# Four edits to the order of work in the scan layer of a decoder trunk: the spread roots go through SBUF, the sums of squares, the casts of y and the turned x change places

## The chip, the cores and the metric

The kernel runs on one core of one Trainium2 chip. The metric is the device time of one execution in microseconds (us), the median of several runs of the same program. The engines are named as the profile names them: PE is the matrix engine (PEld its weight loads), DVE the vector engine, ACT the scalar engine, POOL the general engine, and SP the engine whose queue issues most of the loads.

## What is computed

Two layers of a decoder trunk on 256 tokens of width 1024, all in float32. Each layer is a SwiGLU feed-forward, a token mixer and a second feed-forward, each followed by a layer norm. The first layer's mixer is sparse attention, the second's is a Mamba-2 scan in two chunks of 128 tokens. The change touches the scan layer alone. Cut to what matters there:

```
z, xbc, dt = split(x @ w_in)                    # z: 2048 wide, x: 2048, B and C: 4 groups of 128
xbc = silu(conv(xbc));  xs, b, c = split(xbc)
decay = exp(where(tri, a_cs[l] - a_cs[s], -inf))
y  = (cb * decay) @ (xs * dt)                   # within a chunk, and from chunk 0 to chunk 1
y  = y + xs * d_skip
yz = y * silu(z)                                # 4 groups g of 512 channels
yz = yz * rsqrt(mean(yz ** 2, over the group) + eps)
out = (yz * norm_g) @ w_out
```

## The kernel before, in words

**Precision.** A float32 product is made of three fast ones: every operand is split into a high part H (a cast) and a low part L (the rest), and `mm3` (L565 to L568) adds H·H, H·L and L·H in PSUM. For each weight tile ("unit") a load brings `raw`, ACT casts it to `wh` (L352, or L350 with a scale), and DVE subtracts to make `wl` (L380, L377); for a few units ACT and a DMA that adds (L358, L359) make `wl` instead. Up to ten units are kept ready ahead of PE, and four raws are on their way in this layer.

**The scan layer is turned.** Everything stands with channels on the partitions and tokens along the row. It runs in four stages, g = 0 to 3, one for each group of 512 channels, and each engine carries out its instructions in exactly the order in which the program writes them. To keep PE busy, each stage has up to eight *fillers* f[0] to f[7]: pieces of projection work that depend on nothing in the stage. In stages 0 and 1, f[0] to f[3] compute and convolve the next group's x (`xs_tile`, 24 products, tiles `pxs` or `pmm`), and f[4] to f[7] compute a group of z (`z_tile`, 24 products into one of two PSUM banks `pmm`, freed when ACT has taken silu of it at L1561). In stage 2 there are four x tiles and four output pieces (`out_piece`, 12 products with 512 columns), in stage 3 six output pieces. Between the fillers stand the steps of the stage:

- `x_tok` (L1658 on) transposes x of a group back to tokens on PE (L1666) and multiplies by dt on DVE (L1668); `x_end` multiplies by the decay to the chunk's end (L1672). `decay_cbs` multiplies the three decay tiles M by C·B (L1652).
- `diag` (48 products in the trace, L1685) makes y of the group in two PSUM banks called `ptr`. There are only two such banks; they go round among `diag`, `x_tok`, `root` and `spread`.
- `gate` (DVE, L1695 and L1700) adds the skip and multiplies by silu(z), giving `yc`. `squares` (ACT, L1704) squares it, and `square_sum` (DVE, L1709, L1710) folds the four channel tiles into one.
- `root` sums over the partitions on PE (L1716), copies the two columns out (ACT, L1718) and takes the power -0.5 (POOL, L558).
- One stage later `spread` puts the roots along the rows of a `ptr` bank with two products on PE (L1725), `norm` multiplies `yc` by them on DVE straight out of that bank (L1734) and casts the result to yH on ACT (L1737), and `norm_low` makes yL on DVE (L1741). The output pieces need yH and yL.
- `decay_load` issues the loads of the next stage's decay tiles on POOL's queue, `decay_seg` (DVE, L1639) and `decay_exps` (ACT, L1646) turn them into decays. `flush` issues the silu of the last convolved tile (ACT, L1590); `W.lows()` and `W.pump()` issue the parts of the next weights.

The exponential and the silu each need a table on ACT, so that a table load stands ahead of the exponentials and another ahead of the next silu.

Of the kernel before, what the change touches and what calls it, by code (L numbers as in the profile page):

```python
# [74 lines left out]
def ffn_steps(seven):  # L75
# [3 lines left out]
    while j < NJ:  # L79
        kind, n = ('S', 4) if j in seven else ('R', 1)  # L80
        j += n
# [355 lines left out]
def trunk_kernel(ctx: ExitStack, tc: tile.TileContext, widths, forms, x, ln_g, ln_b, wts, kvg, convp,  # L437
                 dt_bias, a_log, d_skip, norm_g, out):
    nc = tc.nc
# [10 lines left out]
    def nm(s):  # L450
        cnt[0] += 1
        return f"{s}_{cnt[0]}"

    def f4(s):
        return wk.tile([128, 1024], F32, name=nm(s), tag="f4", bufs=12)

    def f2(s):
        return wk.tile([128, 512], F32, name=nm(s), tag="f2", bufs=11)

    def f1(s):  # L460
        return wk.tile([128, 256], F32, name=nm(s), tag="f1", bufs=6)

    def r2(s):
        return wk.tile([128, 512], F32R, name=nm(s), tag="r2", bufs=10)

    def tiny(s, n=32):
        return wk.tile([128, n], F32, name=nm(s), tag=f"tiny{n}", bufs=14 if n == 32 else 4)
# [4 lines left out]
    def pmm():  # L472
        return psum.tile([128, 512], F32, name=nm("pmm"), tag="pmm", bufs=2)
# [11 lines left out]
    def ptr():  # L485
        return psum.tile([128, 512], F32, name=nm("ptr"), tag="ptr", bufs=2)
# [67 lines left out]
    def rsqrt_pool(src):  # L554

        n = src.shape[1]
        o = tiny("rs")
        nc.gpsimd.tensor_tensor(o[:, :n], src, mhalf.to_broadcast([128, n]) if n > 1 else mhalf, op=ALU.pow)  # L558
        return o[:, :n]
# [891 lines left out]
    def ssd(xT, u, ln_i):  # L1451
# [102 lines left out]
        def z_tile(g, i, uu):  # L1554

            if not i:
                zT[g] = f4("zT")
            ps = pmm()
            proj_b(ps[:, :256], xT, uu, False)
            W.free(uu)  # L1560
            nc.scalar.activation(zT[g][:, i * 256:(i + 1) * 256], ps[:, :256], AF.Silu)  # L1561
            W.pump(1)
# [25 lines left out]
        def flush():  # L1588
            while late:
                nc.scalar.activation(*late.pop(0), AF.Silu)  # L1590
# [40 lines left out]
        def hv(ap):  # L1631
            return ap.rearrange("p (h d) -> p h d", h=8)

        def hb(ap, g):
            return ap[:, g * 8:(g + 1) * 8][:, :, None].to_broadcast([128, 8, 64])

        def decay_seg(t, g):

            nc.vector._custom_dve(TENSOR_ADD_SAT, out=M[t].rearrange("p (h l) -> p h l", h=8),  # L1639
                                  in0=M[2 * t].rearrange("p (h l) -> p h l", h=8),  # L1640
                                  in1=acs[t][:, g * 8:(g + 1) * 8][:, :, None].to_broadcast([128, 8, 128]),
                                  s0=0.0, s1=LOWEST)

        def decay_exps():
            for m in (M[0], M[2], M[1]):
                nc.scalar.activation(m, m, AF.Exp)  # L1646
# [7 lines left out]
        yT = {}  # L1654
        y, xe, yc, sq = {}, {}, {}, {}

        def x_tok(t, g):

            if t:
                pt = ptr()  # L1660
            elif g < 3:
                pt = psum.tile([128, 512], F32, name=nm("pxt"), tag="acc11", bufs=1)
            else:
                pt = pmm()
            for i in range(4):
                nc.tensor.transpose(pt[:, i * 128:(i + 1) * 128], xsT[g][i][:, t * 128:(t + 1) * 128], ident)  # L1666
            y[t] = f2("xdt")
            nc.vector.tensor_mul(hv(y[t]), hv(pt), hb(dt[:, t * 32:(t + 1) * 32], g))  # L1668

        def x_end(g):  # L1670
            xe[g] = f2("xe")
            nc.vector.tensor_mul(hv(xe[g]), hv(y[0]), hb(dend, g))  # L1672
# [17 lines left out]
        def gate(g, py):  # L1690
            yc[g] = f4("yc")
            sq[g] = [f2("sq"), f2("sq")]
            for b in range(2):
                for i in (2 * b, 2 * b + 1):
                    nc.vector.scalar_tensor_tensor(yc[g][:, i * 256:(i + 1) * 256], xsT[g][i],  # L1695
                                                   dsk[:, 4 * g + i:4 * g + i + 1],
                                                   py[b][:, (i % 2) * 256:(i % 2 + 1) * 256],
                                                   op0=ALU.mult, op1=ALU.add)
                c = slice(b * 512, (b + 1) * 512)
                nc.vector.tensor_mul(yc[g][:, c], yc[g][:, c], zT[g][:, c])  # L1700
# [5 lines left out]
        def square_sum(g):  # L1706

            a, b = sq[g]
            nc.vector.tensor_add(a, a, b)  # L1709
            nc.vector.scalar_tensor_tensor(b[:, :256], a[:, :256], 4 * RMS_EPS, a[:, 256:], op0=ALU.add, op1=ALU.add)  # L1710

        def root(g):

            pt = ptr()
            for t in range(2):
                nc.tensor.matmul(pt[:, t:t + 1], sq[g][1][:, t * 128:(t + 1) * 128], mean, start=True, stop=True)  # L1716
            ms = tiny("ss")
            nc.scalar.copy(ms[:, :2], pt[:, :2])  # L1718
            return rsqrt_pool(ms[:, :2])

        def spread(rs):

            pt = ptr()
            for t in range(2):
                nc.tensor.matmul(pt[:, t * 128:(t + 1) * 128], rs[:, t:t + 1].to_broadcast([128, 128]), ident,  # L1725
                                 start=True, stop=True)
            return pt[:, :256]

        def norm(g, rs):
            R = spread(rs)  # L1730
            yT[g] = [(r2("yH"), r2("yL")) for _ in range(2)]
            vs = [yc[g][:, b * 512:(b + 1) * 512] for b in range(2)]
            for v in vs:
                nc.vector.tensor_mul(v.rearrange("p (i l) -> p i l", i=2), v.rearrange("p (i l) -> p i l", i=2),  # L1734
                                     R[:, None, :].to_broadcast([128, 2, 256]))
            for (H, L), v in zip(yT[g], vs):
                nc.scalar.copy(H, v)  # L1737

        def norm_low(g):
            for b, (H, L) in enumerate(yT[g]):  # L1740
                nc.vector.tensor_sub(L, yc[g][:, b * 512:(b + 1) * 512], H.bitcast(F32))  # L1741

        def xs_tile(g, i, uu):
            if not i:
                xsT[g] = []
            ps = xbank() if g < 3 else pmm()
            proj_b(ps[:, :256], xT, uu, False)
            W.free(uu)
            if not i % 2:
                pair[0] = f2("xsT")  # L1750
            o = pair[0][:, (i % 2) * 256:(i % 2 + 1) * 256]
            conv(ps, g * 4 + i, o)
            xsT[g].append(o)
            W.pump(1)
# [56 lines left out]
        for g in range(SG):  # L1811
            if g < 2:
                f = [lambda i=i: xs_tile(g + 1, i, u + i) for i in range(4)]
                f += [lambda i=i: z_tile(g + 2, i, u + 4 + i) for i in range(4)]
            elif g == 2:
                x3 = [lambda i=i: xs_tile(3, i, u + 2 * i) for i in range(4)]
                o0 = [lambda i=i: out_piece(i, u + 2 * i + 1) for i in range(4)]
                f = [x3[0], x3[1], o0[0], x3[2], o0[1], x3[3], o0[2], o0[3]]
            else:
                f = [lambda i=i: out_piece(4 + i, u + i) for i in range(6)]  # L1820
            if g:
                x_tok(0, g)
                x_tok(1, g)
            x_end(g)
            decay_cbs(g)
            f[0]()
            if not g:
                z_turn(1)
            if g == 3:
                norm(2, rs)  # L1830
                f[1]()
                py = diag(3)
                gate(3, py)
                squares(3)
                norm_low(2)
                f[2]()
                square_sum(3)
                f[3]()
                rs = root(3)
                f[4]()  # L1840
                norm(3, rs)
                norm_low(3)
                f[5]()
                continue
            f[1]()
            if g:
                norm(g - 1, rs)
            f[2]()
            py = diag(g)
            for t in range(2):  # L1850
                decay_load(t, g + 1)
            if g:
                norm_low(g - 1)
            W.lows()
            gate(g, py)
            f[3]()
            squares(g)
            f[4]()
            flush()
            square_sum(g)  # L1860
            f[5]()
            rs = root(g)
            decay_seg(0, g + 1)
            f[6]()
            flush()
            decay_seg(1, g + 1)
            decay_exps()
            f[7]()
            u += 8
        u += 6  # L1870
# [47 lines left out]
```

## Time and profile before

| what | value |
|---|---|
| median of 3 runs | 1018.83 us (1018.36 to 1019.18) |
| the profiled execution | 1019.94 us |
| its span, first to last instruction | 1018.2 us |
| mean granted clock of PE | 0.993 |
| busy: PE, DVE, ACT, POOL | 98%, 90%, 65%, 10% of the span |
| the four stages of the scan, on PE | about 701 to 814 us of the span |

The trace is of one execution. In the rows of the timeline the columns are start in us, length in us, engine, line, operation, tiles written and read, and in brackets how long the engine had been idle before and whose end it waited for. Matmuls overlap in the pipeline, so that a stretch's length from start to start says more than the sum of its parts. The lines are those of the kernel before.

### The profile page before, as it was taken

The numbers are of one execution on the slowest core, as the hardware profiler recorded it, in microseconds if no ns is written. First come the engines' busy times: TensorE is split into PE (matmuls) and PEld (weight loads), VectorE is DVE, ScalarE is ACT, GpSimd is POOL, SyncE is SP. The second block draws the span as 40 slices with busy tenths as digits, with TensorE's granted clock in tenths as the row PEclk, the third lists the DMA queues.
The fourth block names the chain that finished last, engine by engine and source line by source line (L and its number), as shares of the span: only waits on it lengthen the run. The fifth ranks groups of instructions, "written<-read, shape, count | busy, mean of one in ns | idle before, by whom it ended". The sixth has DMA issues, their size and how long they took to land.

```text
span 1018.2 us, 14875 instructions
## 1 busy us (share of the span) xinstructions
PE 1001.6 (98%) x5445; PEld 851.9 (84%) x5445; DVE 913.2 (90%) x1242; ACT 661.3 (65%) x953; POOL 106.4 (10%) x152
## 2 busy tenths in 40 slices
PE   9999999999999999999999999999989999999996
PEld 7888888898788888888888888999989788888885
DVE  6999998789899999989999998697778999999985
ACT  6776775476657676754777664587757555776670
POOL 0111101100001110000011000150110001010000
PEclk9999999999999999999999999999989999999998
DMA  9989999352638998882999886447686664999751
GB/s 342 281 249 284 297 275 345 105 173 75 214 106 242 253 280 285 267 304 75 266 254 263 278 292 232 164 143 205 205 233 194 225 225 114 292 294 292 207 187 42
DMA packets 64953, 230.66 MB, mean 227 GB/s; under 512 B 7312, under 2 KB 8144, under 8 KB 64880
## 3 DMA queue, kind: packets, MB, share of 16 engines
q1 hardware_dynamic: 52128, 183.95, 50.1%
q0 software_dynamic: 12752, 45.76, 22.5%
q8 instruction: 42, 0.69, 0.3%
q14 instruction: 31, 0.25, 0.1%
HBM read 193.48 MB, written 1.08 MB: 191 GB/s over the span
## 4 chain that ended last, share of the span: by engine, by line
PE 85%; DVE 6%; ACT 3%; issue 2%; DMA 2%; POOL 1%; SPq 0%; DVEq 0%; ACTq 0%; POOLq 0%
PE pmm L566 12%; PE pmm L568 12%; PE pmm L567 12%; PE acc L566 9%; PE acc L568 9%; PE acc L567 9%; PE ptr L567 2%; PE ptr L568 2%; PE ptr L566 2%; DVE wl L380 2%; PE pmm L733 1%; PE ptr L834 1%; DMA raw<-raw 1%; PE ptr L733 1%; PE pxs L566 1%
## 5 line engine op out<-in xcount | busy, mean ns | idle before, releaser
L352 ACT CAST wh<-raw 128x1024 fp32r<-128x1024 f32 (+2 forms) x433 | 430.2, 1039 | 121.4 <-DVE raw L318 78.8
L380 DVE TENSOR_TENSOR wl<-raw,wh 128x1024 fp32r<-128x1024 f32 (+3 forms) x421 | 491.4, 1208 | 14.5 <-ACT wh L352 13.5
L566 PE MATMUL acc<-wh,hH 128*128 128x512 f32 (+1 forms) x352 | 138.0, 392 | 0.0
L567 PE MATMUL acc<-wl,hH 128*128 128x512 f32 (+1 forms) x352 | 136.7, 388 | 0.0
L568 PE MATMUL acc<-wh,hL 128*128 128x512 f32 (+1 forms) x352 | 136.7, 388 | 0.0
L566 PE MATMUL pmm<-wh,xT 128*128 128x512 f32 (+2 forms) x280 | 108.9, 389 | 0.0
L568 PE MATMUL pmm<-wh,xT 128*128 128x512 f32 (+2 forms) x280 | 107.5, 384 | 0.0
L567 PE MATMUL pmm<-wl,xT 128*128 128x512 f32 (+2 forms) x280 | 107.4, 384 | 0.0
L291 POOL DMA_DIRECT2D raw<-raw x59 | 50.8, 876 | 401.2 <-DVE raw L318 233.1
L566 PE MATMUL pmm<-wh,xf 128*128 128x512 f32 x224 | 87.9, 392 | 0.0
L567 PE MATMUL pmm<-wl,xf 128*128 128x512 f32 x224 | 87.3, 390 | 0.2 <-DVE wl L380 0.2
L568 PE MATMUL pmm<-wh,xf 128*128 128x512 f32 x224 | 87.3, 390 | 0.0
L318 DVE TENSOR_TENSOR raw<-raw,raw 128x1024 f32<-128x1024 f32 x69 | 82.9, 1219 | 0.4
L567 PEld LDWEIGHTS acc<-wl,hH 128*128 128x128 f32 x352 | 66.2, 188 | 13.6 <-DVE wl L380 0.8
L568 PEld LDWEIGHTS acc<-wh,hL 128*128 128x128 f32 x352 | 66.1, 188 | 13.7
L566 PEld LDWEIGHTS acc<-wh,hH 128*128 128x128 f32 x352 | 66.2, 188 | 12.9
L568 PEld LDWEIGHTS pmm<-wh,xT 128*128 128x128 f32 x280 | 52.6, 188 | 11.0 <-DVE xT L563 0.9
L567 PEld LDWEIGHTS pmm<-wl,xT 128*128 128x128 f32 x280 | 52.7, 188 | 10.1 <-DVE wl L380 0.8
L566 PEld LDWEIGHTS pmm<-wh,xT 128*128 128x128 f32 x280 | 52.6, 188 | 9.7 <-ACT xT L562 0.4
L567 PEld LDWEIGHTS pmm<-wl,xf 128*128 128x128 f32 x224 | 42.1, 188 | 9.1 <-DVE wl L380 0.6
L568 PEld LDWEIGHTS pmm<-wh,xf 128*128 128x128 f32 x224 | 42.0, 188 | 8.8
L566 PEld LDWEIGHTS pmm<-wh,xf 128*128 128x128 f32 x224 | 42.1, 188 | 8.6
(346 smaller groups left out, 1936.2 us busy)
## 6 DMA issues: line engine op xcount, KB each, us to landing
raw<-in_wts_dram SPq DMA_DIRECT2D x338, 512.0 KB, 5.3
raw<-raw POOLq DMA_DIRECT2D x59, 512.0 KB, 6.1
M<-scr POOLq DMA_DIRECT2D x8, 512.0 KB, 6.2
wl<-raw POOLq DMA_DIRECT2D x8, 512.0 KB, 5.6
lng<-in_ln_g_dram POOLq DMA_DIRECT2D x6, 512.0 KB, 5.6
lnb<-in_ln_b_dram POOLq DMA_DIRECT2D x6, 512.0 KB, 5.3
raw<-in_wts_dram SPq DMA_DIRECT2D x4, 408.0 KB, 5.5
raw<-in_wts_dram SPq DMA_DIRECT2D x4, 256.0 KB, 3.9
```

Source lines behind the costliest of these rows:

```text
L291: self.nc.gpsimd.dma_start(self.raw[r], self.raw[other], accum_op=ALU.add)
L318: self.nc.vector.tensor_add(self.raw[r], self.raw[r], self.raw[other])
L352: nc.scalar.copy(h[:, c:c + n], raw[:, c:c + n])
L380: self.nc.vector.tensor_sub(lo[:, s], raw[:, s], h[:, s].bitcast(F32))
L566: nc.tensor.matmul(ps, lh, rh, start=first, stop=False, skip_group_check=on)
L567: nc.tensor.matmul(ps, lh, rl, start=False, stop=False, skip_group_check=on)
L568: nc.tensor.matmul(ps, ll, rh, start=False, stop=last, skip_group_check=on)
L733: nc.tensor.matmul(ps, H[:, k * 128:(k + 1) * 128], xT.HL[:, k, :], start=k == 0, stop=False)
L834: nc.tensor.transpose(pt[:, i * 256 + t * 128:i * 256 + (t + 1) * 128], h[:, i * 128:(i + 1) * 128], ident)
```

## The change

It makes four edits, all in the scan layer:

1. `spread` copies the roots from the `ptr` bank into a small SBUF tile R on ACT (L1728 of the changed kernel), and DVE multiplies by R instead of by the bank.
2. The casts to yH leave `norm` for a function of their own. In stages 1 and 2 they are issued behind `diag` and the loads of the decay; `norm_low`, which subtracts them, moves behind `gate`. In stage 3 `norm_low(2)` moves behind `square_sum(3)`.
3. `root` of stages 0 to 2 is issued behind f[6] rather than behind f[5].
4. `x_tok` and `x_end` of the next group are issued at the end of a stage, ahead of f[7], rather than at the start of the next one, behind f[7].

```
-            return pt[:, :256]
+            R = f1("R")
+            nc.scalar.copy(R, pt[:, :256])
+            return R
...
-            R = spread(rs)
+            R = rs if rs.shape[1] == 256 else spread(rs)
...
-            for (H, L), v in zip(yT[g], vs):
-                nc.scalar.copy(H, v)
+
+        def norm_high(g):
+            for b, (H, L) in enumerate(yT[g]):
+                nc.scalar.copy(H, yc[g][:, b * 512:(b + 1) * 512])
...
-            if g:
-                x_tok(0, g)
-                x_tok(1, g)
-            x_end(g)
+            if not g:
+                x_end(g)
...
                 norm(2, rs)
+                norm_high(2)
...
                 squares(3)
-                norm_low(2)
                 f[2]()
                 square_sum(3)
+                norm_low(2)
...
             if g:
-                norm_low(g - 1)
+                norm_high(g - 1)
             W.lows()
             gate(g, py)
+            if g:
+                norm_low(g - 1)
             f[3]()
             squares(g)
             f[4]()
             flush()
             square_sum(g)
             f[5]()
-            rs = root(g)
             decay_seg(0, g + 1)
             f[6]()
             flush()
+            rs = root(g)
             decay_seg(1, g + 1)
             decay_exps()
+            x_tok(0, g + 1)
+            x_tok(1, g + 1)
+            x_end(g + 1)
             f[7]()
```

(`rs` always has two columns here, so that `norm` always calls `spread`.)

Three places in the order of the built programs follow. The numbers behind the names tell buffers apart and differ a little between the two programs.

PE, end of stage 1, before: the last products of f[5], the sums over the partitions (L1716), and the first products of f[6].

```order
L566 MATMUL pmm_7602<-xT_6170,wh_7340 128x256
L567 MATMUL pmm_7602<-xT_6170,wh_7340 128x256
L568 MATMUL pmm_7602<-xT_6170,wl_7341 128x256
L1716 MATMUL ptr_7633<-mean,sq_7521 128x1 x2
L566 MATMUL pmm_7641<-xT_6170,wh_7396 128x256
```

PE, end of stage 1, now: the last products of f[6], the sums, the eight transposes of group 2's x (L1666), and the first product of f[7].

```order
L567 MATMUL pmm_7636<-xT_6170,wh_7396 128x256
L568 MATMUL pmm_7636<-xT_6170,wl_7397 128x256
L1716 MATMUL ptr_7668<-mean,sq_7521 128x1 x2
L1666 MATMUL pxt_7679<-ident,xsT_7387 128x128 x2
L1666 MATMUL pxt_7679<-ident,xsT_7473 128x128 x2
L1666 MATMUL ptr_7686<-ident,xsT_7387 128x128 x2
L1666 MATMUL ptr_7686<-ident,xsT_7473 128x128 x2
L566 MATMUL pmm_7695<-xT_6170,wh_7434 128x256
```

So the sums have moved 24 products later, and the transposes 24 products earlier.

DVE, middle of stage 1, before: the product of y with the roots, the convolution of f[2]'s tile (`cv_7474`), low parts of weights (`wl`), yL, and the gate of this stage.

```order
L1734 TENSOR_TENSOR yc_7152<-yc_7152,ptr_7437 128x512 x2
L1598 SCALAR_TENSOR_TENSOR cv_7474<-pxs_7448,convp_sb,cv_7474 128x255
L1598 SCALAR_TENSOR_TENSOR cv_7474<-pxs_7448,convp_sb,cv_7474 128x254
L1598 SCALAR_TENSOR_TENSOR cv_7474<-pxs_7448,convp_sb,cv_7474 128x253
L380 TENSOR_TENSOR wl_7435<-raw_7301,wh_7434 128x1024
L1741 TENSOR_TENSOR yL_7441<-yc_7152,yH_7440 128x512
L1741 TENSOR_TENSOR yL_7443<-yc_7152,yH_7442 128x512
L380 TENSOR_TENSOR wl_7484<-raw_7338,wh_7483 128x1024
L1695 SCALAR_TENSOR_TENSOR yc_7519<-xsT_7023,dsk,ptr_7486 128x256 x2
L1700 TENSOR_TENSOR yc_7519<-yc_7519,zT_7034 128x512
L1695 SCALAR_TENSOR_TENSOR yc_7519<-xsT_7108,dsk,ptr_7487 128x256 x2
L1700 TENSOR_TENSOR yc_7519<-yc_7519,zT_7034 128x512
```

The same place now:

```order
L1736 TENSOR_TENSOR yc_7152<-yc_7152,R_7440 128x512 x2
L1598 SCALAR_TENSOR_TENSOR cv_7474<-pxs_7448,convp_sb,cv_7474 128x255
L1598 SCALAR_TENSOR_TENSOR cv_7474<-pxs_7448,convp_sb,cv_7474 128x254
L1598 SCALAR_TENSOR_TENSOR cv_7474<-pxs_7448,convp_sb,cv_7474 128x253
L380 TENSOR_TENSOR wl_7435<-raw_7294,wh_7434 128x1024
L380 TENSOR_TENSOR wl_7484<-raw_7354,wh_7483 128x1024
L1695 SCALAR_TENSOR_TENSOR yc_7519<-xsT_7023,dsk,ptr_7486 128x256 x2
L1700 TENSOR_TENSOR yc_7519<-yc_7519,zT_7034 128x512
L1695 SCALAR_TENSOR_TENSOR yc_7519<-xsT_7108,dsk,ptr_7487 128x256 x2
L1700 TENSOR_TENSOR yc_7519<-yc_7519,zT_7034 128x512
L1745 TENSOR_TENSOR yL_7443<-yc_7152,yH_7442 128x512
L1745 TENSOR_TENSOR yL_7445<-yc_7152,yH_7444 128x512
```

The two yL stand behind the gate, and the first row reads R instead of a PSUM bank. What stands between that row and the sum of squares has the same length as before; only its order is another.

ACT, middle of stage 1, before: the last weight cast of f[1], the casts of y, and what convolves f[2]'s tile (`cv_7474`).

```order
L352 CAST wh_7434<-raw_7301 128x1024
L1737 CAST yH_7440<-yc_7152 128x512
L1737 CAST yH_7442<-yc_7152 128x512
L1595 ACTIVATE cv_7474<-pxs_7448,convp_sb 128x256
L1590 ACTIVATE xsT_7387<-cv_7426 128x256
L352 CAST wh_7483<-raw_7338 128x1024
```

And now:

```order
L352 CAST wh_7434<-raw_7294 128x1024
L1728 COPY R_7440<-ptr_7437 128x256
L1595 ACTIVATE cv_7474<-pxs_7448,convp_sb 128x256
L1590 ACTIVATE xsT_7387<-cv_7426 128x256
L352 CAST wh_7483<-raw_7354 128x1024
L1741 CAST yH_7442<-yc_7152 128x512
```

The copy of the roots takes the place of the two casts, and the casts stand behind f[2]'s convolution and its weight cast.

More of the change, by code (lines that the diff above doesn't have):

```diff
@@ L1841, in ssd @@
                 norm(3, rs)
+                norm_high(3)
                 norm_low(3)
```

## The prediction

> **What bounds the kernel now.** I read the page first, then the table of the waits of PE between 690 and 815 us, then PE's timeline around each of them, and last the timelines of DVE and ACT, to see why they were late.
>
> ```profile
> span 1018.2 us, 14875 instructions
> PE 1001.6 (98%) x5445; PEld 851.9 (84%) x5445; DVE 913.2 (90%) x1242; ACT 661.3 (65%) x953; POOL 106.4 (10%) x152
> ```
>
> PE is the bound, and it is full almost everywhere. So only stretches in which it stands still, or runs slower than the same work elsewhere, can be won. The waits of PE in the scan have three rows, 5.8 us in all:
>
> ```profile
> PE ptr L1716 <- DVE sq L1710: 3.0, 2, 2.5
> PE ptr L1685 <- DVE yc L1734: 2.4, 2, 1.4
> PE pmm L566 <- ACT zT L1561: 0.4, 1, 0.4
> ```
>
> The windows of PE give what they cost, start to start. The columns are the length of the stretch, PE's busy time with its instructions, the granted clock, and DMA.
>
> ```profile
> 712.24:715.01 2.77, 2.77 (x49) 1.00 0.53 101
> 723.75:729.95 6.20, 6.20 (x54) 1.00 0.76 207
> 729.95:730.75 0.80, 0.80 (x11) 1.00 0.97 343
> 739.98:743.96 3.98, 2.99 (x49) 1.00 0.82 210
> 752.70:755.34 2.64, 0.16 (x3) 1.00 0.60 213
> 755.34:764.63 9.29, 9.29 (x52) 0.63 0.84 222
> 765.42:771.91 6.49, 6.08 (x51) 1.00 0.20 74
> 786.94:792.49 5.55, 5.55 (x26) 1.00 0.82 321
> 799.40:803.95 4.55, 3.16 (x50) 1.00 0.34 115
> 803.95:810.16 6.21, 5.74 (x26) 1.00 0.83 291
> ```
>
> The first three rows are undisturbed: `diag` of stage 0 takes 2.77 us, `root` with two fillers 6.20, the eight transposes 0.80; so is the eighth, two output pieces of stage 2 in 5.55. The same `diag` takes 3.98 in stage 1 and 4.55 in stage 3. In stage 1 `root` comes 2.64 us late (fifth row), and then `root` with its two fillers takes 9.29 instead of 6.20, at a mean granted clock of 0.63 (sixth row). That row is busy throughout: the matmuls themselves are slower.
>
> **Part by part.** The sum is made against the profiled execution, 1019.94 us (its span of 1018.2 and 1.74 around it); that is 1.11 above the median of 1018.83, and I take the difference off the median.
>
> *The roots through SBUF.* In stages 1 and 3 the second bank of `diag` is the one that `spread` filled, and PE stands until DVE has multiplied by it:
>
> ```profile
> 742.50 0.33 PE L1685 MATMUL ptr<-M,xdt 128*64 128x128 f32 x2 [0.99 <-DVE yc L1734]
> 802.49 0.33 PE L1685 MATMUL ptr<-M,xdt 128*64 128x128 f32 x2 [1.39 <-DVE yc L1734]
> 739.74 1.03 ACT L352 CAST wh<-raw 128x1024 fp32r<-128x1024 f32 x1
> 741.79 1.22 ACT L1737 CAST yH<-yc 128x512 fp32r<-128x512 f32 x2 [1.01 <-DVE yc L1734]
> L982 ACT COPY gate<-pmm x5: 373/373/385, 34.2 to 978.6; 128x256 f32<-128x256 f32 x5
> ```
>
> The trace has no copy of the roots; its nearest row is L982, the same shape out of PSUM, 0.37 us. Four of them are 1.5 us on ACT, which idles 1.01 us here ahead of the casts whose place the copy takes. In stage 1 the copy follows the cast that ends at 740.77, so that the bank is free near 741.1; `diag` starts at 739.98 and reaches its second half 1.4 us later. Gain 3.98 - 2.77 = 1.21, at worst 0.9 if the copy is 0.3 late. In stage 3 the cover is as good, but the gain depends on DVE, below.
>
> ```profile
> L1734 DVE TENSOR_TENSOR yc<-yc,ptr x8: 672/678/689, 741.1 to 814.7; 128x512 f32<-128x512 f32 x8
> L1709 DVE TENSOR_TENSOR sq<-sq,sq x4: 683/686/693, 722.2 to 808.9; 128x512 f32<-128x512 f32 x4
> ```
>
> The multiply itself I cost at no change: out of PSUM it takes 678 ns, the same shape out of SBUF alone 686. [...]
>
> *The casts behind the diagonal products, the sums a filler later.* What makes `root` late in stage 1 is DVE, and DVE had itself been held up:
>
> ```profile
> 743.51 1.51 DVE L1598 SCALAR_TENSOR_TENSOR cv<-pxs,convp_sb,cv 128x255 f32<-128x255 f32 x3 [1.15 <-ACT cv L1595]
> ...
> 754.76 0.43 DVE L1710 SCALAR_TENSOR_TENSOR sq<-sq 128x256 f32<-128x256 f32 x1
> 755.34 0.90 PE L1716 MATMUL ptr<-mean,sq 128*128 128x1 f32 x4 [2.48 <-DVE sq L1710]
> ```
>
> The 1.15 us of idle come from ACT: the casts to yH wait for the product, and the convolution of the next tile stands behind them. With the casts moved, DVE goes straight on, and its sum of squares is done at 755.2 - 1.15 = 754.0. yL only changes its place ahead of it. PE, now 1.21 us early, ends f[5] at 752.70 - 1.21 = 751.5 and f[6] 2.9 later (`root` alone is 0.37 from start to start in stage 2, rows below; 6.20 - 0.37 = 5.83 for two fillers), at 754.4. So `root` just doesn't wait: margin 0.3 us. Removed: 2.64. If DVE is half a us later, 0.2 to 0.5 of it stays.
>
> With the stop goes, I think, the slow stretch: the granted clock is 1.00 in the fifth row and 0.63 in the sixth, and PE stood still for 2.48 us just ahead of it. The other stops above, the longest 1.39, have a clock of 1.00 in their rows. Gain 9.29 - 6.20 = 3.09. [...]
>
> *x a filler sooner.* It moves 0.80 us of transposes ahead of f[7], with no work added. On DVE its three products now stand ahead of one `wl`; no weight stands in the table of PE's waits, so I cost that at nothing. Two places lose cover. First, the second x tile of stage 2 reuses the `pmm` bank that f[7] of stage 1 filled, and ACT frees it only behind the exponentials:
>
> ```profile
> 761.60 0.38 ACT L1561 ACTIVATE zT<-pmm 128x256 f32<-128x256 f32 x1 [5.17 <-PE pmm L568]
> ...
> 764.23 2.96 ACT L1646 ACTIVATE M<-M 128x1024 f32<-128x1024 f32 x3
> ...
> 768.51 0.38 ACT L1561 ACTIVATE zT<-pmm 128x256 f32<-128x256 f32 x1
> 768.94 0.39 PE L566 MATMUL pmm<-xT,wh 128*128 128x256 f32 x1 [0.41 <-ACT zT L1561]
> ```
>
> From the end of f[6] to the free bank ACT needs 7.3 us, and 0.15 more for the copy of the sums that now stands between: 7.5, and I allow 0.2 for the last product to end: 7.7. PE reaches that bank after `root`, transposes and two fillers: 0.37 + 0.8 + 5.83 = 7.0. So the wait stays, 0.7 us instead of 6.49 - 5.83 = 0.66: nothing gained. Second, in stage 2 the transposes come nearer to the silu of the last x tile:
>
> ```profile
> 786.57 0.50 PE L1716 MATMUL ptr<-mean,sq 128*128 128x1 f32 x4
> 786.94 0.48 PE L566 MATMUL acc<-wh,yH 128*128 128x512 f32 x1
> 786.77 0.56 ACT L1595 ACTIVATE cv<-pmm,convp_sb 128x256 f32<-128x256 f32 x1 [1.32 <-PE pmm L568]
> 787.53 1.15 ACT L350 ACTIVATE wh<-raw,ng_sb 128x1024 fp32r<-128x1024 f32 x1 [0.20 <-DMA raw<-in_wts_dram]
> 788.59 0.14 ACT L1718 COPY ss<-ptr 128x2 f32<-128x2 f32 x1
> ...
> 789.88 0.40 ACT L1590 ACTIVATE xsT<-cv 128x256 f32<-128x256 f32 x1
> ```
>
> The silu ends 3.7 us after the tile (3.6 without the small copy, which now stands behind it). The transpose that needs it is the fourth: one output piece, `root` and three transposes after the tile, 2.8 + 0.4 + 0.3 = 3.5 us. That is a wait of 0.1; `diag(3)` has 0.2 of such a wait already, for DVE's last decay product, and the one takes the place of the other. I take zero, with 0.5 as the bound against.
>
> *Stage 3.* `diag` and two output pieces lie between 799.40 and `root` at 810.16: 4.55 + 6.21, against 2.77 + 5.55 undisturbed, 2.4 too long. But DVE sets the end here:
>
> ```profile
> 798.74 1.21 DVE L1652 TENSOR_TENSOR M<-M,cbm 128x1024 f32<-128x1024 f32 x1
> ...
> 806.47 1.28 DVE L1741 TENSOR_TENSOR yL<-yc,yH 128x512 fp32r<-128x512 f32 x2
> 807.68 1.28 DVE L377 SCALAR_TENSOR_TENSOR wl<-raw,ng_sb,wh 128x1024 fp32r<-128x1024 f32 x1
> ...
> 809.59 0.42 DVE L1710 SCALAR_TENSOR_TENSOR sq<-sq 128x256 f32<-128x256 f32 x1
> ```
>
> It is busy without a gap from the last decay product to the sum. Only yL leaves that chain, 1.21 us from its start to the next row's. So PE gains 1.2 of the 2.4, and 1.2 of wait is left at `root`. The bounds are 0, if the copy holds up DVE, and 2.4. Behind it the copy lengthens the way from `spread(3)` to the last yL by 0.4, in a stretch in which PE waits for nothing now; between 0 and 0.4 lost, and I take 0.
>
> Sum: 1.21 + 2.64 + 3.09 + 1.2 = 8.1 us. It reaches the end of the kernel, since behind the scan PE is busy all the time, and its work there stays the same:
>
> ```profile
> 813.77:990.00 176.23, 176.23 (x820) 145.96 (x819) 166.58 (x190) 115.29 (x152) 15.13 (x18) 1.00 0.75 234
> ```
>
> So 1018.8 - 8.1 = 1010.7 us; in the profile 1011.8.
>
> **The rivals.**
>
> *A low clock stays in the scan* (0.10): the stop at `root` goes, but what lowers the clock is not that stop alone. For it speaks that two waits (0.7 and 1.2 us) are left and that only one slow stretch is there to judge by; against it, that the stops of 0.99 and 1.39 us have a clock of 1.00 in their rows. Then 3.1 is not won, but slow fillers give ACT's chain ahead of silu(z) its cover, and about 0.5 of the 0.7 of wait there goes: 1010.7 + 3.1 - 0.5 = 1013.3. [...]
>
> *DVE is later than I put it* (0.12): the copy waits behind ACT's casts, `norm` behind the copy, and `root` still stands 1 us in stage 1, while stage 3 gains nothing: 1010.7 + 1 + 1.2 = 1012.9.
>
> *The change does nothing* (0.03): the waits only move to DVE, whose 90% then bound the scan. DVE's gaps in stages 1 and 2 speak against it. 1018.8.
>
> *Slower* (0.03): the early transposes of group 3 wait for a silu that stands behind two weight casts on ACT, and the first of these waited 0.20 us for its load. Each us by which that load is later is a us of PE, and a stop over 2.5 us adds 3.1 of slow clock. From about 5 us of lateness the gain of 8.1 is gone; 7.5 would give 1021.3. The load shifts with the stage, so I hold it for unlikely.
>
> *Better* (0.05): the wait at `root` of stage 3 goes too, 1.2 more: 1009.5. DVE would have to be done earlier there than its row of work allows.
>
> **How the numbers follow.** The forecast has 0.67, with a range of its own from 1010.0 (the 0.7 of wait for silu(z) gone) to 1012.0 (0.3 for a late copy, 0.5 at `root`, 0.5 at the transposes). I hold that for five in six of its cases. The range takes in the better case, the late DVE and the low clock as well: 1009.4 to 1013.6. That holds 0.67 x 5/6 + 0.05 + 0.12 + 0.10, a little over 0.8. A measurement of this kernel tells about 0.2%, 2 us, from no change. The forecast, the low clock, the late DVE and the better case lie below 1016.8: faster 0.94. The change that does nothing: same 0.03. Slower: 0.03.
>
> **What would show it.** In the changed profile: `diag` of stages 1 and 3 near 2.8 us, no wait for the multiply; `root` of stage 1 with under 0.5 us of wait and 1.00 of clock behind it; a wait of 0.5 to 1 for silu(z) ahead of the second x tile of stage 2; a wait near 1.2 at `root` of stage 3. Wrong would be a clock below 1 between 750 and 765 us, a wait of the transposes above 0.5, or a later stretch of the feed-forward that has grown.

## The result, and the profile after

The changed kernel takes 1012.46 us (median of 4 runs, 1011.38 to 1014.12) against 1019.0 for the kernel before, measured beside it; the ratio is 0.9933, with a 95% interval of 0.991 to 0.9955. A second set of runs, told below, gave 1012.04 (5 runs). Both lie within the range of the prediction, 1009.4 to 1013.6, and 1.3 to 1.8 us above its forecast of 1010.7; both lie a little above the range that the forecast had of its own, 1010.0 to 1012.0. The profiled execution took 1011.38 us.

From the page of the changed kernel, its span and the busy time of PE:

```profile
span 1009.7 us, 14871 instructions
PE 998.3 (99%) x5445; PEld 849.0 (84%) x5445; DVE 913.0 (90%) x1242; ACT 661.8 (66%) x957; POOL 107.4 (11%) x152
```

The span is 8.5 us shorter, with the same 5445 matmuls. DVE and ACT work as long as before (913.0 us against 913.2, 661.8 against 661.3): nothing was taken off them, only put elsewhere. The waits of PE in the scan, 690 to 815 us, of the changed kernel:

```profile
PE ptr L1716 <- DVE sq L1710: 0.9, 1, 0.9
PE pmm L566 <- ACT zT L1561: 0.4, 1, 0.4
```

Of 5.8 us of waits 1.3 are left. The row of `diag` waiting for DVE's multiply is gone, and `root` waits once (stage 3) instead of twice. What the stretches take now, from the windows of PE in the changed kernel (length, PE's busy time, granted clock, DMA):

```profile
739.10:741.87 2.77, 2.77 (x50) 1.00 0.96 234
753.49:753.85 0.36, 0.36 (x6) 1.00 1.14 307
754.68:760.39 5.71, 5.71 (x50) 1.00 0.48 126
757.53:764.05 6.52, 6.11 (x51) 1.00 0.54 186
782.65:788.21 5.56, 5.56 (x28) 1.00 0.60 197
791.50:794.48 2.98, 2.98 (x50) 1.00 0.12 14
794.48:801.11 6.63, 5.73 (x27) 1.00 0.85 313
804.77:990.00 185.23, 185.05 (x856) 1.00 0.73 225
```

They are, in this order: `diag` of stage 1, 2.77 us instead of 3.98; `root` of stage 1, 0.36 from its start to the next product, without the 2.64 that stood ahead of it; the work behind the transposes that follow (f[7], and nearly all of f[0] of stage 2), now at a clock of 1.00, where the work behind `root` had 0.63; f[0] and f[1] of stage 2 with the wait for silu(z) between them; two output pieces of stage 2, undisturbed as before; `diag` of stage 3, 2.98 instead of 4.55; the two pieces behind it up to `root`, 6.63, of which PE works 5.73; and the feed-forward behind the scan, where PE is busy for all but 0.18 us of 185.

Five rows of the timelines of ACT, DVE and PE in the changed kernel show why (`...` stands for rows left out):

```profile
739.43 0.36 ACT L1728 COPY R<-ptr 128x256 f32<-128x256 f32 x1
...
739.84 1.29 DVE L1736 TENSOR_TENSOR yc<-yc,R 128x512 f32<-128x512 f32 x2
...
752.49 0.42 DVE L1710 SCALAR_TENSOR_TENSOR sq<-sq 128x256 f32<-128x256 f32 x1
...
753.49 0.50 PE L1716 MATMUL ptr<-mean,sq 128*128 128x1 f32 x4
...
801.11 0.58 PE L1716 MATMUL ptr<-mean,sq 128*128 128x1 f32 x4 [0.90 <-DVE sq L1710]
```

The copy is done at 739.8, 0.7 us after `diag` begins; PE needs the bank 1.4 us after. The sum of squares of stage 1 is done at 752.9, and PE gets to it at 753.5.

### The profile page after: what moved, and what is told of

Same layout as the page of the kernel before. It is cut to its first block, busy times and chain, and to the rows that moved or that the text cites. A ratio compares the mean times of both kernels' runs of the same rounds, so it can differ in the third digit from the quotient of the medians.

```text
span 1009.7 us, 14871 instructions
## 1 busy us (share of the span) xinstructions
PE 998.3 (99%) x5445; PEld 849.0 (84%) x5445; DVE 913.0 (90%) x1242; ACT 661.8 (66%) x957; POOL 107.4 (11%) x152
## 4 chain that ended last, share of the span: by engine, by line
PE 83%; DVE 8%; ACT 2%; DMA 2%; issue 2%; POOL 1%; SPq 0%; DVEq 0%; POOLq 0%; ACTq 0%
PE pmm L568 11%; PE pmm L566 11%; PE pmm L567 11%; PE acc L566 8%; PE acc L567 8%; PE acc L568 8%; DVE wl L380 3%; PE ptr L567 3%; PE ptr L568 3%; PE ptr L566 3%; PE pmm L733 2%; PE ptr L834 1%; DMA raw<-raw 1%; PE ptr L733 1%; PE pxs L566 1%
```

## The experiments

Ten kernels ran, the changed one once more among them, in three sets, each beside runs of the kernel before. Theory: DVE's chain sets both `root` of stage 1 and `root` of stage 3, and a stop of PE brings the low clock. The main rival was that the low clock belongs to the place or the load and not to the stop.

### One edit at a time

**The copy alone**, in the kernel before:

```
+            R = f1("R")
+            nc.scalar.copy(R, pt[:, :256])
+            return R
```

> The kernel before with the first edit alone: the roots are copied out of PSUM, nothing moves. Chain theory (what ends at the sums is set by DVE, and stops of PE ahead of it only trade places): diag of stages 1 and 3 falls to about 2.8 us, but the sums of both stages come no earlier, so the stop at the sums of stage 1 grows from 2.5 to about 3.7 us and the one of stage 3 from 0.5 to about 2; the low clock stays. Time within 0.5 us of before, or up to 2 us more if the longer stops bring more slow clock. Rival (each wait that goes is won by itself): 1.2 + 1.6 = 2.8 us faster.

Measured: 1020.92 us (11 runs), ratio 1.0022 (1.0014 to 1.0031). Slower by 0.2%. Its table of PE's waits and its windows:

```profile
PE ptr L1716 <- DVE sq L1710: 5.8, 2, 3.7
```

```profile
740.16:742.93 2.77, 2.77 (x49) 1.00 0.71 217
799.26:802.19 2.93, 2.93 (x49) 1.00 0.11 13
802.19:810.02 7.83, 5.74 (x26) 1.00 0.85 308
```

The copy does just what it should: `diag` takes 2.77 and 2.93. But PE only comes sooner to a `root` whose sum DVE delivers no sooner. In stage 1 the wait grows from 2.48 to 3.7 us. In stage 3 the way from `diag` to `root` is 2.93 + 7.83 = 10.76, to the hundredth what it was before (4.55 + 6.21). So in both stages DVE sets the end, and the copy's gain turned into wait. Behind the two longer stops the clock is low for longer: in this profile three stretches of 3.41 us have a granted clock of 0.50, two behind the stop of stage 1 (753.92 to 760.74) and one behind that of stage 3 (811.95 to 815.36), where the kernel before has two, and its span is 1.5 us longer (1019.7 against 1018.2). The middle span is 1.9 longer (1019.1 against 1017.2); that this is the clock as well is likely, but not shown run by run.

**The sums a filler later alone:**

```
-            rs = root(g)
             decay_seg(0, g + 1)
             f[6]()
             flush()
+            rs = root(g)
```

> The kernel before with the third edit alone: the sums over the partitions stand behind f[6]. Chain theory with the clock hanging on the stop: no stop at the sums of stage 1 (2.64 us) and no low clock behind it (3.1), about 0.3 more wait for silu(z), diag as long as before: 5.4 us faster. Rival (the low clock has another cause than that stop): 2.4 us faster, with a granted clock below 1 still in stage 1 or 2.

Measured: 1014.65 us (5 runs), ratio 0.9952 (0.9939 to 0.9965), 4.3 us less. One more filler covers the whole wait of stage 1, and the clock behind `root` is 1.00 (756.16 to 759.48). Of PE's waits at `root` only that of stage 3 is left:

```profile
PE ptr L1716 <- DVE sq L1710: 0.5, 1, 0.5
```

The 4.3 stand 1.1 below the 5.4 expected; that 1.1 comes back below.

**The casts alone** (`norm_high` behind `diag`, `norm_low` behind `gate`, and in stage 3 `norm_low(2)` behind `square_sum(3)`):

> The kernel before with the second edit alone: the casts of y behind the diagonal products, yL behind the gate. Chain theory: DVE's sum of stage 1 is done 1.15 us earlier, so that a stop of about 1.4 us is left there; if stops of that length leave the clock alone (as 1.39 us did before), the slow stretch goes too, and in stage 3 the sums come 1.2 us earlier: 1.15 + 3.1 + 1.2 = 5.4 us faster, diag as slow as before. If a stop of 1.4 us still lowers the clock: 2.4 us faster.

Measured: 1017.25 us (8 runs), ratio 0.998 (0.997 to 0.999), 1.7 us less. The windows of PE around `diag` and `root` of stage 3 in this kernel:

```profile
797.55:802.09 4.54, 3.15 (x50) 1.00 0.33 108
802.09:807.68 5.59, 5.59 (x27) 1.00 0.86 299
```

Here `root` of stage 3 doesn't wait at all, but `diag` waits as before: 10.13 instead of 10.76, a gain of 0.63 where 1.2 was expected. In stage 1 the casts alone shorten the stop from 2.48 to 1.44 us, and the second reading of the expectation, that this still lowers the clock, was the nearer one.

**x a filler sooner alone:**

> The kernel before with the fourth edit alone: x of the next group is turned ahead of f[7]. Chain theory: nothing on PE's path hangs on it, the waits for the sums, for diag and for silu(z) stay: within 0.5 us of before. Rival (it gives DVE its products earlier and so shortens DVE's chain): 0.6 to 2 us faster, with an earlier end of the decay products in stages 1 to 3.

Measured: 1019.05 us (12 runs), ratio 0.9999 (0.999 to 1.0007). Nothing, as expected. The ratios of the four, one by one, add up to -0.5%; together they bring -0.7%. The copy, a loss by itself, seems to pay once the two edits around DVE let PE use the time. That is read from the windows of `diag`: no run took the copy, or the casts, alone out of the changed kernel.

### What lowers the clock

The profile of the kernel with only x moved had an unexpected side: PE stood for 2.48 us ahead of `root` of stage 1, as long as in the kernel before, and the clock stayed at 1.00. So I cut the traces into steps. The low stretches in the scan last 6.82 us (the kernel before, 755.43 to 762.25) or 3.41 (only the casts moved), one or two times the same step, and the two low stretches of the kernel before, in the scan and at the end of the program, begin 256.00 us apart (755.43 and 1011.43), 75 times 3.413. That the clock goes by such steps throughout is my reading of these lengths. Laid from the edges of the low stretches through each trace, the steps lie elsewhere against the stop in each of three profiles. First the kernel before, then that with only x moved, then that with only the casts, in windows of one step:

```profile
752.01:755.43 3.42, 0.94 (x9) 1.00 0.56 187
755.43:758.84 3.41, 3.41 (x17) 0.50 1.02 262
758.84:762.25 3.41, 3.41 (x18) 0.50 0.86 205
762.25:765.66 3.41, 3.41 (x31) 1.00 0.50 159
799.80:803.21 3.41, 2.02 (x36) 1.00 0.27 77
803.21:806.62 3.41, 3.41 (x28) 1.00 0.76 274
```

```profile
750.34:753.75 3.41, 2.05 (x18) 1.00 0.87 311
753.75:757.16 3.41, 2.29 (x19) 1.00 0.78 216
757.16:760.57 3.41, 3.41 (x32) 1.00 0.96 229
```

```profile
751.87:755.28 3.41, 1.97 (x17) 1.00 0.88 287
755.29:758.70 3.41, 3.41 (x18) 0.50 0.94 213
758.70:762.11 3.41, 3.41 (x30) 1.00 0.36 74
```

In the kernel before the whole stop falls into one step: 2.48 us of 3.42 idle, and the next two steps have a clock of 0.50. With only x moved the edge of a step falls into the middle of the same stop, 1.36 us idle on one side and 1.12 on the other, and 1.00 follows. With only the casts moved the stop is much shorter, but all in one step, 1.44 us, and one low step follows. In these three the length of the stop alone doesn't decide, then: 2.48 us were followed by 0.50 once and once by 1.00. The idle time within one step does separate them: 2.48 and 1.44 us against 1.36 and 1.12. That it was the place of the edge in this one run that spared the kernel with x moved, and not its edit, is what its twelve spans suggest: two are 1015.1 and 1015.2, the others 1016.5 to 1018.8, a spread like that of the kernel before. The eight spans with only the casts moved fall into two groups, 1013.6 to 1014.4 and 1015.3 to 1015.8, as if the shorter stop cost a low step in some runs only; there is one profile, so this isn't shown.

To take the stop away without moving `root`, PE got junk products to work on while it waited, right ahead of the sums of stage 1 in the kernel before (20 in one kernel, 10 in the other):

```
+            if g == 1:
+                for _ in range(20):
+                    nc.tensor.matmul(pt[:, 128:384], xT.H[:, 0, :128], xT.H[:, 0, :], start=True, stop=True)
             for t in range(2):
```

> The kernel before, and in stage 1 PE gets 20 products of 128x256 that nothing reads, right ahead of the sums of root(1), so that it works through the 2.5 us in which it stood. The sums come when they did. Theory: the clock record goes in steps of 3.413 us (6.827 is two, the single one in the run with only the casts moved is one), and a step in which PE stands for some 1.4 us or more is followed by one or two at 0.5; where the steps lie differs from run to run, so that the stop costs nothing, 1.5 or 3.1 us. With PE busy there is no low step: span 1015.1 in every run, as in the one profile of the kernel with only x moved, which had the stop and no low step; that is 2.0 less than the 1017.1 at the middle of the runs of the kernel before, median near 1016.9, mean clock 0.997 or more, and spans that agree within 1 us where the kernel before has 3.7. Rival (the low clock comes with this place of the program, or with its load, and not with the stop): span 1016 to 1019 as before, median 1018.9.

> As the run before this one with 10 products: PE stands for about 1.25 us of the 2.5, which is at most 0.37 of a step of 3.413 us. Theory: the shortest stop that a low step followed so far is 1.44 us (only the casts moved, in about half of its runs), and one of 1.39 in stage 3 of the kernel before had none; so no low step, span 1015.1, median 1016.9, as with 20 products. Rival (any stop of about 1 us lowers the clock in some runs): between, median 1017.5 to 1018.5, with spans up to 1018. Rival (the stop does not matter): 1018.9.

Measured: with 20 products 1016.93 us (9 runs), ratio 0.9978 (0.9968 to 0.9988); with 10 products 1017.43 (11 runs), ratio 0.9982 (0.9973 to 0.9991). The step with the wait and the one behind it, first with 20 products, then with 10:

```profile
752.70:756.11 3.41, 3.33 (x29) 1.00 0.68 227
756.11:759.52 3.41, 3.41 (x31) 1.00 1.03 231
```

```profile
752.45:755.86 3.41, 2.12 (x18) 1.00 0.69 223
755.87:759.28 3.41, 3.41 (x30) 1.00 1.06 237
```

Useless work made the kernel quicker, with the place and the load as they were: the rival is out. `root` comes as late as ever, and only the idle time of PE is gone. Ten products leave 1.29 us of it in one step, and that is still harmless in the profile; the middle span is 1015.7 against 1015.2, so that for a few of its runs a low step isn't excluded. Over all runs measured the spans agree with the theory: 62 runs of the kernel before spread from 1015.2 to 1018.9 with the middle at 1017.2, while with 20 products eight of nine lie between 1014.8 and 1015.5. So by these middles, 1017.2 and 1015.2, the low clock costs the *middle* run of the kernel before an estimated 2.0 us, and not the 3.09 that its profile shows.

### The whole change again, and without single edits

**The changed kernel once more:**

> The changed kernel once more, for more of its runs. Theory: its stops are 0.4 and 0.9 us, so no run has a low step in the scan: spans of 1009.5 to 1010.8 in all, 7.2 below the middle of the runs before and not 8.1, because the middle run before had one low step where the profiled one had two; median 1011.8. Rival (a low clock stays in some runs): spans up to 1012.5 with a mean clock of 0.996 or less, median 1012.5 or more.

Measured: 1012.04 us (5 runs, 1011.34 to 1012.83), ratio 0.9926 (0.9914 to 0.9939). The nine spans of both sets lie between 1009.6 and 1011.1, the middle at 1010.3, 6.9 below that of the kernel before. Two of the four runs first measured had 3.3 and 3.4 us outside the span where most others have 1.7 to 2.0; that lifts their median.

**Without x sooner**, the rest of the change kept:

> The changed kernel with x turned where it was before. Theory (turning x sooner moves 0.80 us of PE's work and nothing waits for it; the wait for silu(z) and the waits of stage 3 stay): no change from the changed kernel beyond 0.5 us, span 1010.3, median 1012.0, no low clock. Rival (the early x is what lets a later wait go, or gives DVE a product too early): 1 to 2 us apart, with a stop of PE in the scan that the changed kernel has not.

Measured: 1012.33 us (5 runs), ratio 0.9938 (0.9926 to 0.995), middle span 1010.0. The same as the changed kernel: the fourth edit is worth nothing here, alone or with the others.

**With the sums back ahead of the seventh filler**, the rest kept:

> The changed kernel with the sums back in front of the seventh filler; copy, casts and x stay changed. Theory: DVE's sums are done at 752.9 and PE reaches root(1) at 750.6, so it stands 2.3 us, as in the kernel before; 0.7 of step 1's gain and all of the clock's is lost again, since a stop of 2.3 us puts over 1.42 us of idle into some step of 3.413 in nearly every run. 2.3 of stop, 1.5 to 3.1 of low clock, less 0.6 of the wait for silu(z) that slow fillers cover: 3.2 to 4.8 more than the changed kernel, span 1013.5 to 1015, median 1015.3 to 1016.8, mean clock 0.996 or less in most runs. Rival (with the copy and the casts moved the sums no longer come late): within 1 us of the changed kernel.

Measured: 1016.61 us (12 runs), ratio 0.9974 (0.9964 to 0.9985); spans 1012.8 to 1017.1, the middle at 1014.65, 4.3 above the changed kernel. In its profile:

```profile
752.39:755.80 3.41, 1.35 (x12) 1.00 0.94 285
755.80:759.21 3.41, 3.41 (x19) 0.50 0.84 216
759.22:762.63 3.41, 3.41 (x31) 1.00 0.52 144
```

PE stands again, 2.06 us of one step, and one low step follows. The whole stop is 2.66 us long; the other 0.6 lie in the step before. With copy, casts and x in place the sums still come too late for the old order; the third edit carries most of the gain.

**A version that goes on.** The first x tile of stage 2 takes the accumulator bank that is free there, so that the second has a free `pmm` bank and not the one that waits for silu(z), and in stage 3 one weight split leaves DVE's chain ahead of the sum of squares:

```
-            ps = xbank() if g < 3 else pmm()
+            if g == 3 and not i:
+                ps = psum.tile([128, 512], F32, name=nm("pxs"), tag="acc10", bufs=1)
+            else:
+                ps = xbank() if g < 3 else pmm()
...
-        def out_piece(k, uu):
+        def out_piece(k, uu, pump=1):
...
-            W.pump(1)
+            if pump:
+                W.pump(1)
...
-                f = [lambda i=i: out_piece(4 + i, u + i) for i in range(6)]
+                f = [lambda i=i: out_piece(4 + i, u + i, i != 1) for i in range(6)]
...
                 norm_low(2)
+                W.pump(1)
```

> The changed kernel with its two last waits attacked: the first x tile of stage 2 takes the free accumulator bank and does not wait for silu(z) (0.6), and in stage 3 one weight split of DVE (1.28 us) goes behind the lows of y, so that the sum of squares is done 1.2 us sooner than where root(3) waits 0.9. Theory (both waits are set by what they wait for, and behind them PE is the bound): 1.5 less than the changed kernel, span 1008.2 to 1009. Rival (the bank only moves the wait to the next tile, and the late split holds up the next weight): span 1009.5 to 1011, no gain; the profile then shows a wait for wl or for xT.

Measured: 1010.77 us (4 runs, 1010.44 to 1010.89), ratio to the kernel before 0.9911 (0.9898 to 0.9925). Its spans, 1008.6 to 1009.2, lie all below those of the changed kernel. The windows of PE over f[7] of stage 1 and the first two fillers of stage 2, and from the end of `diag` to `root` in stage 3:

```profile
755.95:764.66 8.71, 8.71 (x75) 1.00 0.61 176
795.09:800.66 5.57, 5.57 (x26) 1.00 0.92 346
```

Against 9.37 (754.68 to 764.05) and 6.63 in the changed kernel both are full, and its table of PE's waits in the scan is empty. It gained 0.66 + 1.06 there, where 1.5 was expected, and 1.3 in the middle span; it beats both kernels.

## Why the prediction was right, and where it was too large

- **The copy: right.** 1.21 predicted in stage 1, 3.98 - 2.77 = 1.21 measured. The run with the copy alone (ratio 1.0022) adds that it was no gain where DVE came late at `root`.
- **The multiply at no change: right.** Its group in the changed kernel, duration of one as minimum, median and maximum in ns:

```profile
L1736 DVE TENSOR_TENSOR yc<-yc,R x8: 682/684/693, 739.8 to 806.1; 128x512 f32<-128x512 f32 x8
```

  684 ns out of SBUF against 678 out of PSUM: in this pair the source in PSUM cost no extra time.
- **The stop at `root` of stage 1: right.** All of the 2.64 went, with a margin of 0.6 instead of 0.3: the sum was done at 752.9.
- **The wait for silu(z): right.** It stays, with 6.52 instead of 6.49 for the same two fillers. The version that takes the free bank shows that it is the bank: 0.66 went with it.
- **The transposes of group 3: right.** No wait.
- **Stage 3: right.** 1.2 predicted; 10.76 became 2.98 + 6.63 = 9.61, so 1.15, with 0.90 of wait left at `root` where I had 1.2. That DVE sets the end there is shown by the copy alone (10.76, no gain) and by the last version (5.57, no wait).
- **Behind `root` of stage 3: taken at zero, and not quite zero.** The prediction put between 0 and 0.4 on the copy's way to the last yL, took 0, and held the work behind the scan for unchanged. From `root` of stage 3 to the end of its last product PE takes 200.07 us in this profile and 199.57 in the second one of the changed kernel, where it took 199.22. It goes with the copy: without x sooner it is 199.56 and with the sums back 199.64, while all six profiles without the copy have 199.14 to 199.29. What comes behind PE's end is 0.36 shorter, 8.48 instead of 8.84. So of the 9.05 us that `root` of stage 3 comes sooner the span keeps 8.5. Where on that way the time goes stays open.
- **The slow clock: the cause right, the size off.** This is the step that failed: "Gain 9.29 - 6.20 = 3.09." It is what the profiled execution lost, and the pair of profiles did gain about the whole sum: `root` of stage 3 starts 9.05 us sooner, of which 0.84 is the scan's earlier start (`diag` of stage 0 at 711.40 instead of 712.24), so 8.2 against 8.1. But I took the sum off the median, and the middle run of the kernel before loses 2.0 there. With 2.0 the sum is 7.0, and the middle spans differ by 6.9. The kernel with the sums alone missed by the same 1.1. The profiled run stood 1.11 above the median; the 1.1 by which its slow clock exceeds that of the middle run is about the same, and I hadn't asked whether a stop costs alike in each run. So the measured medians came out above the forecast's own range, and the wider range holds them because it takes in the late DVE and the low clock, of which neither came; that much of the hit is luck.

The rival "a low clock stays in the scan" gave 1013.3, not far from the median; the windows read in the scan of the two profiles of the changed kernel are all at 1.00, and its nine spans lie within 1.5 us. In these traces stops of 1.44 us (only the casts moved) and 2.48 (the kernel before) were followed by a clock of 0.50, and the 2.48 us that fell into two steps (only x moved) by 1.00. My reading that the idle time within one step decides fits the low stretches of 3.41 and 6.82 us in the scan, the edges of the steps, which lie elsewhere in each of these profiles, and the spread of the spans, which goes from 3.7 us (62 runs of the kernel before) to 1.7 (nine with 20 products) when the stop is filled; the end of the program, below, it does not explain.

## What to carry to other kernels

The gain that I took from the low clock, 3.09 us, was that of one execution; the middle run had an estimated 2.0. So cut the trace into steps, look how much of one step the stop fills, and take the middle of many runs for its price. The copy that frees a bank sooner didn't pay here while the same late engine set the next wait: alone it made that stop longer (2.48 to 3.7 us in stage 1) and the kernel slower (ratio 1.0022). Where PE waited here for a chain on another engine, moving the waiting instruction one piece of independent work later was worth more (4.3 us) than shortening a link of the chain (1.7).

## What the runs showed of the hardware that was not expected

- In the scan of these traces the clock of PE went to 0.50 for one or two steps of 3.41 us, and the idle time within the step ahead separates the cases. Steps with 1.36 us idle (only x moved) and 1.39 (stage 3 of the kernel before, 3.41 - 2.02 above) were followed by 1.00; steps with 1.44, 1.49, 2.06, 2.09 (the copy alone, stage 1) and 2.48 by 0.50. So among these the border lies between 1.39 and 1.44 us, 41 to 42% of a step. The 1.49 are in the run with the copy alone, in stage 3:

```profile
808.53:811.94 3.41, 1.92 (x11) 1.00 0.84 285
811.95:815.36 3.41, 3.41 (x12) 0.50 0.84 294
```

- At the end of the program, where PE does its last product, the same border doesn't hold in two profiles. In the second profile of the changed kernel 1.60 us of idle are followed by a step at 1.00, and only the one after that is low:

```profile
1000.01:1003.42 3.41, 1.81 (x16) 1.00 0.00 0
1003.42:1006.83 3.41, 0.00 (x0) 1.00 0.23 84
1006.83:1010.24 3.41, 0.00 (x0) 0.50 0.23 74
```

  The run with the sums back has 1.85 us there, also with 1.00 behind it; the kernel before has 2.04, with 0.50 behind it. So PE's idle time in one step doesn't separate all the cases, and what else counts stays open. (These low steps cost nothing: PE has no work left, 0.00 us in the one above.)
- After 2.48 us in one step two low steps followed, although PE was busy through the first of them; after 1.44, 1.49 and 2.06 it was one. (After the 2.09 there were two as well, but PE stood for 1.61 us of the first.) Why is open: no run was made on it.
- Twenty products that nothing reads made the kernel 2 us quicker (middle span 1015.2 against 1017.2): in that step of the profile PE stood for 0.08 us instead of 2.48, and the clock behind it was 1.00.
